# A ranked start, one pause in the state-space queue, and work moved between engines in a two-layer encoder kernel

## The chip, the cores and the metric

The kernel runs on 1 core of one Trainium2 chip. The time is the device time of one execution, in microseconds (us); a number of a kernel is the median over its runs. All data enter and leave in float32. The engines are called TensorE (PE in the rows), VectorE (DVE), ScalarE (ACT), GpSimd (POOL) and SyncE (SP); SyncE starts most DMA transfers, GpSimd starts some.

## The reference

Two sequences, 512 and 256 tokens of width 2048, pass through two layers. The even layer runs a state-space mixer (two directions, 64 groups of 16 channels, 64 states) with a gated linear unit, beside an attention of 8 heads over 2 key/value heads; the odd layer runs 16 heads of attention in which three windows are mixed. Each ends with an out-projection, a residual and a layer norm.

```python
def trunk(x):
    ...
    for layer in range(DEPTH):
        i = layer // 2
        if layer % 2 == 0:
            h = x @ even_w_in[i]
            a_u, a_g, q, k, v, b_g = jnp.split(h, EVEN_SPLITS, axis=-1)
            ya = _s5_mixer(a_u, ...)
            yb = _axial_gqa(q, k, v, attn_q_norm[i], attn_k_norm[i], row, col)
            y = jnp.concatenate([ya * jax.nn.silu(a_g), yb * jax.nn.silu(b_g)], axis=-1) @ even_w_out[i]
        else:
            h = x @ odd_w_in[i]
            q, k, v, g = jnp.split(h, 4, axis=-1)
            y = (_dilated_mixture(q, k, v, pos) * jax.nn.silu(g)) @ odd_w_out[i]
        x = _layernorm(DN_ALPHA * x + y, ln_g[layer], ln_b[layer])
    return x
y_prompt = trunk(x_prompt)
y_sample = trunk(x_sample)
```

In the mixer, `y = gelu(state-space output)`, then `y * sigmoid(y @ glu_w + glu_b)`. The attention normalises q and k per head, rotates them (rope), takes a softmax over all keys and sums the values.

## The kernel before

All 768 tokens are kept on chip with features on the 128 partitions, so a projection runs over weight blocks of 128 x 512 and streams 384 (or 256, 512) columns per matmul. Float32 operands are split into a rounded high part (a cast on ScalarE, L441 or L447) and a low part (the difference, on VectorE or GpSimd, L442 or L448); each product is three matmuls, high by high, high by low and low by high.

The order of the work is written by hand. Projections (`proj_f`, L536; `proj_t`, L580) call `fill` after every block of matmuls: 24 of 384 columns in `proj_f` (6 with `fine`), 36 of 256 columns in `proj_t`. A fill takes the next entry of a queue `c.q` (or a `nop`, which is a pause of one fill) and everything that `later` has set down for that count. What is in the queue runs between the matmuls: TensorE's part of it stands in TensorE's program at that place, and VectorE, ScalarE and GpSimd get theirs through their own in-order programs. `flush` empties the queue at once. A scheduler puts each engine's instructions in order by a modelled time and a rank; `high_priority(n)` raises the rank of what is created in it, `issue_after(i)` holds an instruction behind another.

The stages that the change touches, in order of time:

- **Start** (`load_x`, `before`): x is transposed on TensorE (`ps_x`), cast on ScalarE (`xh`) and its low parts are taken on VectorE (`xl`), while both engines also work out the state-space tables (`pi`, `ui`, `tt`, L137 to L160).
- **State space** (`Ssm`, eight batches b): `inward` makes `swb`, `bb`, `swbb` and `win`, `outward` makes `swc` and `ca`; `ends` turns them on TensorE (`ps_w`, `ps_s`), `cmat` gives `cst` (through `ps_c`), `lags` gives `ps_k`, `scan` is a long chain on VectorE that ends with the two copies to `xb` (L394), and `outs` (`ps_y`, L409 to L412) uses the scan one batch later. `gate` multiplies a projection's two banks into `gt` on VectorE (L682).
- **k and q blocks** (`qk_block`): norm on VectorE, rope as sine products (L669, VectorE), cosine products (L672, GpSimd) and their sum (L673, VectorE), then transposes on TensorE (`ps_q`, L648). Key, value and query of a head are then loaded and split (`load_kv`, `Head0.load`).
- **First attention** beside the glu products: a `step` of the attention (scores `ps_sc`, softmax on VectorE and ScalarE, transposes `ps_pt`, values `ps_o`) is one queue entry.
- **Start of the second layer**: the layer-normed rows z are turned (`four`), sums and differences of quarters are formed (`sums`, L1208), and the first products of a seven-product scheme run alone (`sv.alone`).
- **Last out-projection**: the last heads of the second attention run between its matmuls; each k block of the mixed heads is loaded (`md`) and split (`mix_in`, L1447), the gates (`g`, Tanh, L1439) are loaded through `pd`, and the first 256 columns of the residual (`res0`) are loaded from `nd` and get the layer norm's gain and offset (`residual1`, L1350).

## Time and profile before

| | |
|---|---|
| median of 3 runs | 2634.8 us (2634.49 to 2635.05) |
| profiled execution | 2632.97 us |
| its span in the trace | 2631.2 us |
| TensorE busy | 2541.3 us, 97% |
| VectorE busy | 1787.2 us, 68% |
| ScalarE busy | 1050.0 us, 40% |
| GpSimd busy | 772.5 us, 29% |
[...]

Busy time is summed per engine over the span. [...] The trace has about 90 us in which TensorE does nothing, most of it in a few waits.

### The profile page before, as it was taken

How to read it: one execution, taken by the hardware profiler on the slowest of the kernel's cores; microseconds unless marked ns; L12 is line 12 of the kernel's file. 1: busy time of each engine (PE TensorE's matmuls, PEld its weight loads, DVE VectorE, ACT ScalarE, POOL GpSimd, SP SyncE). 2: the span in 40 equal slices, each digit the busy share in tenths (PEclk: the TensorE clock that was granted, in tenths of full speed). 3: DMA queues.
4: the chain of work that ended last, by engine and by line, in shares of the span. 5: the costliest groups of instructions: out<-in, count | busy, mean ns of one | idle time of the engine just before them, and what ended most of it. 6: DMA issues, size and time to landing. Idle time of an engine off the chain costs nothing.

```text
span 2631.2 us, 41939 instructions
## 1 busy us (share of the span) xinstructions
PE 2541.3 (97%) x15632; PEld 2432.2 (92%) x15632; DVE 1787.2 (68%) x3516; ACT 1050.0 (40%) x2102; POOL 772.5 (29%) x641
## 2 busy tenths in 40 slices
PE   7999999999999999998999999999999999989996
PEld 7999999999988998888999999999999999988886
DVE  6488998878445542238866666778788878763437
ACT  4322233222237731117433333456555656651111
POOL 2555666645564420004000000012212212244404
PEclk9999999999999999999999999999999999989998
DMA  5433333332354462125443444454544454456222
GB/s 154 124 88 99 96 98 97 102 88 71 110 150 141 142 207 64 64 89 165 138 131 124 129 126 127 137 117 111 119 115 109 112 117 113 101 163 196 77 74 106
DMA packets 353451, 308.59 MB, mean 117 GB/s; under 512 B 60384, under 2 KB 305120, under 8 KB 352352
## 3 DMA queue, kind: packets, MB, share of 16 engines
q1 hardware_dynamic: 333200, 265.83, 33.3%
q0 software_dynamic: 10688, 36.71, 6.9%
q10 hardware_dynamic: 9360, 3.38, 0.7%
q8 instruction: 123, 2.02, 0.3%
q14 instruction: 80, 0.66, 0.1%
HBM read 232.10 MB, written 67.44 MB: 114 GB/s over the span
## 4 chain that ended last, share of the span: by engine, by line
PE 70%; DVE 16%; DMA 4%; issue 3%; POOL 2%; ACT 1%; SPq 0%; DVEq 0%; POOLq 0%; ACTq 0%
PE pt L580 23%; PE ps_y L753 12%; PE ps_z L753 8%; PE ps_x L753 8%; PE pa L536 4%; PE pb L536 4%; PE ps_o L885 3%; PE ps_sc L843 2%; DMA res<-pd 2%; PE ps_pt L872 2%; DVE wl L442 1%; DVE tmpv L227 1%; DVE xs L370 1%; PE ps_y L410 1%; DVE sc_sw L369 1%
## 5 line engine op out<-in xcount | busy, mean ns | idle before, releaser
L441 ACT CAST wh<-wr 128x512 fp32r<-128x512 f32 x348 | 216.3, 622 | 715.3 <-PE pt L580 391.5
L580 PE MATMUL pt<-wh,xh 128*128 128x256 f32 (+1 forms) x1392 | 458.8, 330 | 0.9 <-DVE z L898 0.8
L580 PE MATMUL pt<-wl,xh 128*128 128x256 f32 (+1 forms) x1392 | 456.1, 328 | 0.0
L580 PE MATMUL pt<-wh,xl 128*128 128x256 f32 (+1 forms) x1392 | 455.9, 327 | 0.0
L442 POOL TENSOR_TENSOR wl<-wr,wh 128x512 fp32r<-128x512 f32 x176 | 245.1, 1398 | 532.7 <-ACT wh L441 470.0
L442 DVE TENSOR_TENSOR wl<-wr,wh 128x512 fp32r<-128x512 f32 x172 | 145.8, 849 | 257.0 <-ACT wh L441 256.4
L580 PEld LDWEIGHTS pt<-wh,xh 128*128 128x128 f32 x1392 | 265.8, 191 | 25.0 <-issue 2.5
L580 PEld LDWEIGHTS pt<-wl,xh 128*128 128x128 f32 x1392 | 265.8, 191 | 22.3
L580 PEld LDWEIGHTS pt<-wh,xl 128*128 128x128 f32 x1392 | 265.5, 191 | 22.3
L753 PE MATMUL ps_y<-xh,wh 128*128 128x384 f32 x768 | 260.0, 339 | 0.0
L753 PE MATMUL ps_y<-xl,wh 128*128 128x384 f32 x768 | 257.1, 335 | 0.9 <-DVE xl L1208 0.9
L753 PE MATMUL ps_y<-xh,wl 128*128 128x384 f32 x768 | 257.0, 335 | 0.0
L441 ACT CAST wh<-b 128x512 fp32r<-128x512 f32 x248 | 151.6, 619 | 184.4 <-PE ps_z L753 91.5
L442 DVE TENSOR_TENSOR wl<-b,wh 128x512 fp32r<-128x512 f32 x248 | 170.2, 688 | 38.4 <-ACT wh L441 38.2
L753 PE MATMUL ps_x<-xh,wh 128*128 128x384 f32 x512 | 176.1, 344 | 7.5 <-ACT early L761 6.1
L753 PE MATMUL ps_z<-xh,wh 128*128 128x384 f32 x512 | 174.1, 340 | 0.0
L753 PE MATMUL ps_x<-xh,wl 128*128 128x384 f32 x512 | 172.0, 336 | 0.0
L753 PE MATMUL ps_x<-xl,wh 128*128 128x384 f32 x512 | 171.9, 336 | 0.0
L753 PE MATMUL ps_z<-xh,wl 128*128 128x384 f32 x512 | 171.4, 335 | 0.0
L753 PE MATMUL ps_z<-xl,wh 128*128 128x384 f32 x512 | 171.1, 334 | 0.0
L536 PE MATMUL pa<-xh,wh 128*128 128x384 f32 x448 | 158.3, 354 | 4.4 <-ACT xh L447 3.3
L536 PE MATMUL pa<-xh,wl 128*128 128x384 f32 x448 | 151.5, 338 | 0.6 <-POOL wl L442 0.4
(355 smaller groups left out, 6374.7 us busy)
## 6 DMA issues: line engine op xcount, KB each, us to landing
b<-in_odd_w_in_dram SPq DMA_DIRECT2D x256, 256.0 KB, 3.0
wr<-in_even_w_in_dram SPq DMA_DIRECT2D x144, 256.0 KB, 3.3
pd<-z SPq DMA_DIRECT2D x56, 384.0 KB, 2.5
wr<-in_even_w_out_dram SPq DMA_DIRECT2D x64, 256.0 KB, 2.6
wr<-in_odd_w_out_dram SPq DMA_DIRECT2D x64, 256.0 KB, 3.0
res<-pd POOLq DMA_DIRECT2D x16, 768.0 KB, 6.9
res<-pd POOLq DMA_DIRECT2D x16, 576.0 KB, 6.4
nd<-z POOLq DMA_DIRECT2D x12, 512.0 KB, 4.2
```

Source lines behind the costliest of these rows:

```text
L227: e.tensor_tensor(out=tmp, in0=pt(9 + j), in1=xt(sx), op=ALU.mult)
L369: v.tensor_tensor(out=sw, in0=sw, in1=bc(ai), op=ALU.mult)
L370: v.tensor_tensor(out=x1, in0=x1, in1=sw, op=ALU.add)
L410: nc.tensor.matmul(o, s.ca[:, 0, g, 1:9].rearrange("p j c -> p (j c)"), s.xs[:, 0:8, :, g].rearrange("p j r -> p r j"), start=False, stop= ...
L441: cast = nc.scalar.copy(hi, src)
L442: (eng or nc.gpsimd).tensor_tensor(out=lo, in0=src, in1=hi.bitcast(F32), op=ALU.subtract)
L536: nc.tensor.matmul(out[n][s][:, 0:HALF], wt[:, j], xt[k][:, HALF * s:HALF * s + HALF], start=k == k0 and i == 0, stop=k == nk - 1 and i == 2)
L580: nc.tensor.matmul(view[t], xt[k][:, tok], wt[:, j], start=first and i == 0 and ti % per == 0, stop=last and i == 2 and ends)
L753: nc.tensor.matmul(ps, w[:, k], x(k), start=i < 3 and k == j == 0, stop=k == 3 and j == 2, skip_group_check=i >= 3)
L843: nc.tensor.matmul(s, a[:, qs], b[:, ks], start=j == 0, stop=j == 2)
L872: nc.tensor.transpose(ps[:, 128 * j:128 * j + 128], seq.ps[i][:, 128 * j:128 * j + 128], c.ident)
L885: nc.tensor.matmul(o, a, b[:, j], start=j == 0 and x == 0, stop=j == nt - 1 and x == 2)
```

## The change

In the order of the program:

1. Start: the cast and the low part of x in `load_x` are ranked 400 higher.
2. State space: in batch 1 a `nop` is put into the queue behind `ends[1]`, so that all later entries of the state space run one fill later than before against the projections.
3. Before the k and q blocks the `nop` ahead of `tables_in` goes; the cosine products move from GpSimd to VectorE (two of 128 x 256 in each of 15 blocks); the last q block is transposed at fills 2, 3, 4 instead of 1, 2, 3; the low parts of the first key, value and query go from GpSimd to VectorE.
4. First attention: the two fills ahead of the glu loop go.
5. Second layer's start: the products with index 0 run for all four n first, then those with index 3; the last token tile's `four` and `sums` are ranked 400 higher, and the second half of the sums is issued after the first half's last low part.
6. Last out-projection: the gates of the last pair come at fills 5 and 8 instead of 4 and 5, and their Tanh is issued after the attention's cast; the mixed heads are loaded into five buffers of their own four blocks ahead, apart from their splits; the residual's two operations go to VectorE and to block k = 4, its load to k = 9; the extra fills stand at k = 1, 3, 9, 11, 13 and the flush at k = 4.

```diff
 def split_ps(nc, src, hi, lo):
-    nc.scalar.copy(hi, src)
+    cast = nc.scalar.copy(hi, src)
...
+                with c.tc.high_priority(400):
+                    split_ps(nc, ps[:, 0:HALF], c.xh[k][:, tok], c.xl[k][:, tok])
...
-            nc.gpsimd.tensor_tensor(out=o, in0=u, in1=cg[:, 2 * i + tt].unsqueeze(1).to_broadcast([128, 2, 128]), op=ALU.mult)
+            nc.vector.tensor_tensor(out=o, in0=u, in1=cg[:, 2 * i + tt].unsqueeze(1).to_broadcast([128, 2, 128]), op=ALU.mult)
...
-                        ends[1],
+                        ends[1]]
+                    if b == 1:
+                        c.q.append(nop)
+                    c.q += [
...
-            c.q += [nop] + [tables_in, k_part, nop, nop, o[0], o[1], o[2], o[3]]
+            c.q += [tables_in, k_part, nop, nop, o[0], o[1], o[2], o[3]]
...
-                load_split(pk, kd[kv], *k, 3)
-                load_split(pk, vd[kv].rearrange("p t f -> p (t f)"), *v, 3)
+                eng = None if kv else nc.vector
+                load_split(pk, kd[kv], *k, 3, eng)
+                load_split(pk, vd[kv].rearrange("p t f -> p (t f)"), *v, 3, eng)
...
-            q_block(3, at=(1, 2, 3))
+            q_block(3, at=(2, 3, 4))
...
-            fill(c, 2)
             for f in range(8):
                 ps = proj_f(c, [(glu_w[0], 128 * f)], 8, fine=True)[0]
...
                     def more():
-                        tt(a12, a12, a11, ALU.subtract)
+                        with tc.issue_after(last[-1].ins):
+                            tt(a12, a12, a11, ALU.subtract)
                         split(parts[2:])
...
+                else:
+                    c.q += [lambda f=f: ranked(f) for f in ks((4, 0)) + [sums]]
+                    late.extend(ks((8, 12)))
...
-                for n in range(n_first):
-                    for i in (0, 3):
+                for i in (0, 3):
+                    for n in range(n_first):
                         sv.alone(n, i, lambda: fill(c, 2))
...
-                        later(c, 4 + i, lambda i=i: gate_sb(blocks[i], two[i], i))
+                        later(c, 4 + i if n < 31 else 5 + 3 * i, lambda i=i: gate_sb(blocks[i], two[i], i))
...
-                nc.scalar.activation(out=g, in_=t, func=AF.Tanh, scale=0.5)
+                with tc.issue_after(att.cast):
+                    nc.scalar.activation(out=g, in_=t, func=AF.Tanh, scale=0.5)
...
+            def mix_load(k, raw=None):
+                if k < 15:
+                    mixed[k] = pm.tile([128, TOK], F32, tag="mi", name="mi", bufs=5) if raw is None else raw
+                    nc.sync.dma_start(mixed[k], md[k])
...
             def mix_in(k):
                 if k < 15:
-                    raw = pc.tile([128, 4, HALF], F32, tag="res", name="res", bufs=3).rearrange("p a n -> p (a n)")[:, 0:TOK]
-                    nc.sync.dma_start(raw, md[k])
-                    split_sb(nc, raw, c.xh[k], c.xl[k], nc.vector)
+                    with tc.issue_after(att.cast):
+                        split_sb(nc, mixed[k], c.xh[k], c.xl[k], nc.vector)
...
-            nc.sync.dma_start(res0, nd[:, :, 0:256])
-            residual1(pc, res0, 0)
...
-            for k in order1[:3]:
+            for k in order1[:2]:
+                mix_load(k, first[:, TOK * k:TOK * k + TOK])
                 mix_in(k)
+            for k in order1[2:4]:
+                mix_load(k)
...
-                m = order1.index(k) + 3
-                if k in (1, 3, 9):
+                m = order1.index(k)
+                if k in (1, 3, 9, 11, 13):
                     fill(c)
-                if k == 10:
+                if m < 12:
+                    mix_load(order1[m + 4])
+                if m < 14:
+                    mix_in(order1[m + 2])
+                if k == 9:
+                    nc.sync.dma_start(res0, nd[:, :, 0:256])
+                if k == 4:
                     flush(c)
-                if m < 16:
-                    mix_in(order1[m])
+                    residual1(pm, res0, 0, nc.vector)
```

What this does to the engines' programs is seen at three places. The first is VectorE behind the first scan, whose end is the copy to `xb`; `gt` is the gate, `swc` and `tmpv` belong to the output matrix, `swb`, `bb`, `swbb` and `win` to the input matrix of the next batch. Before:

```order
L394 COPY xb<-xs 128x8x32
L682 SCALAR_TENSOR_TENSOR gt<-gt,pa 128x384
L682 SCALAR_TENSOR_TENSOR gt<-gt,pb 128x384
L258 STREAM_SHUFFLE swc<-cst 128x256
L227 TENSOR_TENSOR tmpv<-st,swc 128x576
L236 STREAM_SHUFFLE swb<-bst 128x128
L243 TENSOR_TENSOR bb<-st,bst 128x256
L242 TENSOR_TENSOR bb_1993<-st,swb 128x256
L244 TENSOR_TENSOR bb<-bb,bb_1993 128x256
L246 STREAM_SHUFFLE swbb<-bb 128x256
L228 TENSOR_TENSOR win<-st,bb 128x512 x2
```

Now:

```order
L394 COPY xb<-xs 128x8x32
L684 SCALAR_TENSOR_TENSOR gt<-gt,pa 128x384
L684 SCALAR_TENSOR_TENSOR gt<-gt,pb 128x384
L236 STREAM_SHUFFLE swb<-bst 128x128
L243 TENSOR_TENSOR bb<-st,bst 128x256
L242 TENSOR_TENSOR bb_2023<-st,swb 128x256
L244 TENSOR_TENSOR bb<-bb,bb_2023 128x256
L246 STREAM_SHUFFLE swbb<-bb 128x256
L258 STREAM_SHUFFLE swc<-cst 128x256
L228 TENSOR_TENSOR win<-st,bb 128x512
L227 TENSOR_TENSOR tmpv<-st,swc 128x576
L228 TENSOR_TENSOR win<-st,bb 128x512
```

The five operations from `swb` to `swbb` stood behind `swc` and `tmpv`; now they stand ahead of both.

The second place is VectorE behind the next scan (L391 is the scan's last sum); the same names, and in the batches after it the rows read the same way. Before:

```order
L391 TENSOR_TENSOR xs<-xs,sc_f_2258 128x7x48
L394 COPY xb<-xs 128x8x32
L682 SCALAR_TENSOR_TENSOR gt<-gt,pa 128x384
L682 SCALAR_TENSOR_TENSOR gt<-gt,pb 128x384
L236 STREAM_SHUFFLE swb<-bst 128x128
L243 TENSOR_TENSOR bb<-st,bst 128x256
L242 TENSOR_TENSOR bb_2707<-st,swb 128x256
L244 TENSOR_TENSOR bb<-bb,bb_2707 128x256
L246 STREAM_SHUFFLE swbb<-bb 128x256
L228 TENSOR_TENSOR win<-st,bb 128x512 x2
L258 STREAM_SHUFFLE swc<-cst 128x256
L227 TENSOR_TENSOR tmpv<-st,swc 128x576
```

Now:

```order
L391 TENSOR_TENSOR xs<-xs,sc_f_2295 128x7x48
L684 SCALAR_TENSOR_TENSOR gt<-gt,pa 128x384
L394 COPY xb<-xs 128x8x32
L684 SCALAR_TENSOR_TENSOR gt<-gt,pb 128x384
L242 TENSOR_TENSOR bb_2737<-st,swb 128x256
L243 TENSOR_TENSOR bb<-st,bst 128x256
L244 TENSOR_TENSOR bb<-bb,bb_2737 128x256
L246 STREAM_SHUFFLE swbb<-bb 128x256
L228 TENSOR_TENSOR win<-st,bb 128x512 x2
L236 STREAM_SHUFFLE swb<-bst 128x128
L258 STREAM_SHUFFLE swc<-cst 128x256
L227 TENSOR_TENSOR tmpv<-st,swc 128x576
```

One product of the gate now stands between the scan's last sum and the second copy to `xb`; the `swb` that stood ahead of `bb` was taken an earlier turn, and the next batch's `swb` stands in front of `swc`.

The third place is ScalarE in the last out-projection: `g` is the Tanh of a gate, `pth` the attention's cast, `pp` its softmax, `xh` the cast of a mixed head's block, `o` the copy of an attention output. Before:

```order
L1466 ACTIVATE o_24528<-ps_o 128x256
L447 CAST pth<-ps_pt 128x2x128
L854 ACTIVATE pp<-pp,sst 128x512
L1439 ACTIVATE g_24808<-res 128x768
L441 CAST xh<-res 128x768
L447 CAST pth<-ps_pt 128x2x128
L1439 ACTIVATE g_24852<-res 128x768
L852 ACTIVATE pp,sst<-pp,sst 128x512
L441 CAST xh<-res 128x768
L854 ACTIVATE pp<-pp,sst 128x512
L441 CAST wh<-wr 128x512
```

Now, at the first of the two gates:

```order
L447 CAST pth<-ps_pt 128x4x128
L856 ACTIVATE pp<-pp,sst 128x512
L441 CAST xh<-mi 128x768
L441 CAST wh<-wr 128x512
L447 CAST pth<-ps_pt 128x4x128
L1454 ACTIVATE g_24842<-res 128x768
L854 ACTIVATE pp,sst<-pp,sst 128x512
L441 CAST xh<-mi 128x768
L856 ACTIVATE pp<-pp,sst 128x512
L854 ACTIVATE pp,sst<-pp,sst 128x256
L1487 ACTIVATE o_24898<-ps_o 128x256
```

The gates stood ahead of the next `pth` and, the second, right behind it; now the first of them stands behind two more softmax steps, and the mixed heads' casts read their own buffers `mi`.

## Rows read from the trace of the kernel before

**Rows 1.** which waits TensorE had: us in total, times, the longest
```profile
PE ps_q L648 <- DVE qr L673: 10.9, 4, 5.7
PE ps_y L410 <- DVE xs L391: 8.2, 3, 5.9
PE ps_o L885 <- ACT pth L447: 7.1, 2, 5.3
PE ps_x L753 <- ACT early L761: 6.1, 3, 3.5
...
PE ps_pt L872 <- ACT pp L854: 4.9, 2, 3.7
PE ps_sc L843 <- DVE kl L442: 4.7, 4, 3.3
PE ps_x L603 <- DVE xl L448: 4.4, 2, 2.8
PE pa L536 <- ACT xh L447: 3.3, 1, 3.3
```

**Rows 2.** Stretches: us; busy PE, PEld, DVE, ACT, POOL; granted clock; DMA share; GB/s
```profile
20.00:45.00 25.00, 17.34 (x107) 16.14 (x105) 24.04 (x90) 12.56 (x29) 9.13 (x10) 0.93 0.54 121
160.00:245.00 85.00, 77.00 (x480) 76.16 (x479) 72.66 (x168) 22.73 (x45) 40.53 (x29) 0.92 0.39 102
270.00:290.00 20.00, 20.00 (x118) 20.00 (x117) 19.39 (x64) 4.23 (x9) 8.67 (x7) 1.00 0.48 119
626.00:633.00 7.00, 7.00 (x61) 7.00 (x60) 5.74 (x10) 1.49 (x3) 5.41 (x7) 1.00 0.14 40
640.00:656.00 16.00, 10.35 (x77) 10.14 (x77) 11.81 (x20) 4.67 (x9) 10.76 (x12) 0.89 0.28 73
745.00:802.00 57.00, 46.82 (x253) 44.45 (x253) 29.71 (x48) 27.99 (x53) 32.39 (x24) 0.92 0.51 162
1210.00:1250.00 40.00, 33.00 (x180) 31.24 (x179) 36.18 (x54) 27.14 (x63) 12.51 (x12) 0.91 0.56 168
2312.00:2360.00 48.00, 37.16 (x244) 35.30 (x243) 31.44 (x49) 29.13 (x58) 22.50 (x15) 0.86 0.60 177
```

**Rows 3.** timeline of ScalarE, start of the kernel: start, us, line, out<-in, count, wait
```profile
36.39 2.52 ACT L151 ACTIVATE tt<-pi 64x576 f32<-64x576 f32 x4 [5.12 <-DVE pi L143]
```

**Rows 4.** timeline of VectorE and TensorE around the state-space batches
```profile
176.50 0.01 DVE L258 LOAD_MASK_SELECT swc<-cst  x1 [6.86 <-ACT cst L220]
...
177.70 0.30 DVE L236 STREAM_SHUFFLE swb<-bst 128x128 f32<-128x128 f32 x1
...
179.97 0.44 DVE L246 STREAM_SHUFFLE swbb<-bb 128x256 f32<-128x256 f32 x1
...
365.48 0.58 PE L410 MATMUL ps_y<-xs,ca 128*128 128x96 f32 x2 [0.24 <-DVE xs L391]
365.76 0.55 DVE L682 SCALAR_TENSOR_TENSOR gt<-gt,pa 128x384 f32<-128x384 f32 x1
```

**Rows 5.** k and q blocks: operations by line and shape, 675 to 692 us
```profile
L669 DVE TENSOR_TENSOR qsq<-qn,qks 128x128 f32<-128x128 f32 x12 | 7.4, 674 | 0.0
L672 POOL TENSOR_TENSOR qr<-qn,qkc 128x256 f32<-128x256 f32 x6 | 4.6, 785 | 2.2 <-DVE qn L663 2.2
```

**Rows 6.** timeline around the last scan, and VectorE before the last q block
```profile
609.38 0.39 DVE L394 COPY xb<-xs 128x256 f32<-128x256 f32 x1
...
614.80 0.36 PE L409 MATMUL ps_y<-ug,mtoep 128*128 128x96 f32 x2
...
745.31 0.69 DVE L660 TENSOR_REDUCE qss<-qsq 128x4 f32<-128x512 f32 x1 [17.05 <-ACT qsq L658]
```

**Rows 7.** timeline at the head of the last out-projection
```profile
2314.83 5.48 DVE L442 TENSOR_TENSOR ql<-res,qh 128x768 fp32r<-128x768 f32 x1 [1.17 <-ACT qh L441]
2315.97 3.52 POOL L1350 TENSOR_TENSOR res<-res,lrow 128x1536 f32<-128x1536 f32 x1
...
2334.95 0.84 ACT L1439 ACTIVATE g<-res 128x768 f32<-128x768 f32 x1 [3.33 <-DMA res<-pd]
```

## Prediction of the time after the change

> **What bounds the kernel now.** TensorE works 2541.3 of the span's 2631.2 us (the table), so there is little to be had but its waits and its half clock. I read its waits first [rows 1]. The reader is to see eight groups that make 49.6 us, nearly all of them in stretches that the change touches (of the 4.7 only the longest, 3.3), and that each has one or two long waits. Then the same stretches with the granted clock [rows 2]. One less the clock, times the length, is what a stretch loses to the half level: 0.07 x 25 = 1.8 us at the start, 0.08 x 85 = 6.8 in the state space, 0.11 x 16 = 1.8 and 0.08 x 57 = 4.6 around the q blocks and the first attention, 0.09 x 40 = 3.6 at the second layer's start, 0.14 x 48 = 6.7 in the last out-projection: 25.3 us. Two stretches without waits have the full level, 1.00 [rows 2]. So the clock falls where TensorE has waited, and a wait that goes can give its loss back. At stake are some 73 us, no more. Last I read the timeline at each place, for what ends the wait [rows 3 to 7].
>
> Prices of a fill: 24 matmuls of 384 columns at 20.00 / 118 = 0.17 us make 4.1 us; 36 of 256 columns at 7.00 / 61 = 0.115 also 4.1; six of the glu products 1.0 [rows 2].
>
> **Part 1, start.** Three waits, 4.4 in two and 3.3 [rows 1]. The last four casts of x stood behind four multiplies of 2.52 / 4 = 0.63 us [rows 3] and now stand behind three of them; the low parts move by about as much. But VectorE is busy 24.04 of 25 us here [rows 2]: the rank makes no time, it puts table work behind x. Nothing gained to all 7.7 gained; I take -2.0, three times the 0.63, with the clock unchanged.
>
> **Part 2, state space.** (a) The first `ps_y` waits 5.9 us for the scan [rows 1]. The scan does not move, TensorE has one fill more to do until then: -4.1, and 1.8 stays. (b) Of 8.2 some 2.1 are left for the second `ps_y` (0.24 is a third). VectorE stood idle 6.86 us ahead of `swc`, and did `swb` to `swbb` behind it, 177.70 to 180.41 [rows 4]; now these 2.7 us fall into the idle time: the wait goes, -2.0 (0 if `bst` lands late). (c) Clock: with one wait gone and one cut to 1.8 I count 4.4 of the 6.8. (d) In five later batches a gate product of 0.55 us slips between the scan's last sum and the second copy to `xb`. There is nothing to spare: in one of these batches TensorE already waits 0.24 for the scan [rows 4]. So 5 x 0.5 = +2.5 (0 to 2.8). Together -8.0.
>
> **Part 3, k and q blocks.** By TensorE's program the last batch's `ps_s` now stands behind 2652 projection matmuls (2616 before) and its `ps_y` behind 2877 (2904 before): 63 fewer lie between, 7.2 us. The scan was done at 609.77 and used at 614.80 [rows 6], 5.0 us to spare: a new wait of 2.2 (0 to 3.5). The wait of 5.7 at the first q block's end is that of the same VectorE chain, which starts one fill later. On it go two cosine products a block: not shown on VectorE; between less than nothing (L669, 0.67 us on the mean for 128 columns, is stretched beside GpSimd's products) and GpSimd's 0.785 [rows 5]; I take 0.4, near the copy of 256 columns to `xb`, 0.39 [rows 6], and as much back. So little changes: -1.0 with the clock, between -7.5 (both gone) and +4.
>
> [...]
>
> The last q block has the other 5.2 of the 10.9 [rows 1]. Its three transposes come one fill, 4.1 us, later, while VectorE ends as before: all 5.2 go, and 1.4 of the clock: -6.6. The three low parts cost nothing: even at 5.48 us each, the slowest of their width [rows 7], they would fill 16.4 of the 17.05 us in which VectorE stood idle [rows 6].
>
> **Part 4, first attention.** `ps_pt` waits 4.9 us in two [rows 1] for a softmax without matmuls beside it. Without the two fills, two of the steps get six glu matmuls between them: -2.0, and half of the 3.2 us of clock that the q block leaves: -1.5. The attention ends two fills later, with fewer glu products to cover its last values: +1.4 (0 to 2.0). Together -2.1.
>
> **Part 5, second layer's start.** The 6.1 us in three waits [rows 1] are those of the products with index 3, which now come later. But VectorE is busy 36.18 of 40 us [rows 2] and the next products need its low parts: TensorE waits there in their place. I take -2.0 (0 to -9.7, the waits and the clock).
>
> **Part 6, last out-projection.** (a) `ps_sc` waits 3.3 us: `ql` took 5.48 us on VectorE around the residual's 3.52 on GpSimd [rows 7], and `kl` came behind it. The residual leaves that place. But the first mixed block is now cast behind `kh` and a softmax step, and TensorE needs it for its first matmul: by two casts of the 0.84 of `g`'s width [rows 7] about 1.8 of wait, -1.5. (b) ScalarE stood 3.33 us for a gate's load [rows 7] with `pth` behind it, and TensorE 5.3 [rows 1]. The gates come later, behind `pth`: -5.2. (c) The other wait for `pth`, 1.8, has a whole half block of 18 matmuls in front of it now: -1.8. (d) The residual on VectorE, 1536 columns twice: between 2.2 us (four times the 0.55 of 384 columns [rows 4]) and GpSimd's 3.52; 2.2 taken. Behind it stands the softmax of the next step, and two half blocks of 18 matmuls, 4.1 us, cover most: +1.0. (e) Clock: 4.9 of 6.7. Together -12.4.
>
> [...]
>
> **Sum.** -2.0 - 8.0 - 1.0 - 6.6 - 2.1 - 2.0 - 12.4 = -34.1 us. The profiled execution took 2632.97 us (1.8 around the span) and would take 2598.9. The median lies 1.8 above the profiled execution: 2600.7.
>
> **Rivals.** First, handed back: VectorE's chains set the end in parts 2 to 5, and every half-clock stretch stays. Then -1 at the start, -4.1 - 1.5 + 2.5 in the state space, -5.2 + 2.2 in the q blocks, nothing in parts 4 and 5, -7.5 in the last: -14.6, 2620. For it: VectorE's busy shares [rows 2]; against it: long waits that end on a load or on GpSimd have nothing to do with these chains.
>
> Second, the out-projection keeps its waits: the residual's load now stands behind seven loads on SyncE, and if it lands late VectorE stops ahead of a softmax; the gain of 12.4 is lost: -21.7, 2613. For it: one load held ScalarE 3.33 us [rows 7]. Against it: the first softmax behind it is due a half block later.
>
> Third, slower: from the third batch on `swb` stands in front of `swc` and waits for `bst`, which SyncE loads only after `bb` has read the buffer; and the chain has nothing to spare [rows 4]. In six batches the loss is six times what VectorE's idle time there does not cover; from 5.7 us a batch on it eats the 34.1. At the 6.86 us that VectorE once waited at this place [rows 4] it is +41.2 - 34.1 = +7.1: 2642. Against it: the wait was for `cst`, and `ca` behind it waits for `ps_y` anyway.
>
> **How the numbers follow.** The forecast has 0.58, the first rival 0.20, the second 0.12, the third 0.07, and 0.03 that parts cancel to no change. About 0.2%, 5.3 us, is what a measurement of this kernel can tell from no change. A quarter of the first rival falls within it: faster 0.58 + 0.15 + 0.12 = 0.85, same 0.08, slower 0.07. The range goes up to 2622, just past the first rival, and down to 2584: with the unknown bounds at parts 1, 3 and 5 in the kernel's favour by half (2.9 + 3.2 + 3.9) and the rest of the clock in parts 2 and 6 (4.2) and in part 4 another 1.5.
>
> **What would show it.** In the trace after: the first `ps_y` waits under 2 us and the second not at all, `swbb` ends ahead of `swc`; `ps_y` of the last batch waits about 2; the last q block's transposes and the `pth` behind the gates wait for nothing; the first matmul of the last out-projection waits for `xh`; the clock at 1.00 around the second `ps_y` and the last q block. I am wrong if the waits of rows 1 come back under other names with the same sum, or if `ps_y` waits for the scan in each batch.

## The result and the profile after

The changed kernel took 2607.04 us (median of four runs, 2604.1 to 2610.74), the kernel before 2634.64 beside it (2631.41 to 2635.05). The ratio is 0.9899, with a 95% interval of 0.9881 to 0.9916: 27.6 us less, where 2600.7 us had been forecast, in a range of 2584 to 2622. The profiled execution took 2610.74 us, the slowest of the four, with a span of 2608.7. So the two traces differ by 22.5 us and the medians by 27.6; terms of one or two microseconds can't be read from the medians, and I read them from the traces, stage by stage. Of the 22.5 us, 5.3 are TensorE's busy time (2541.3 before, 2536.0 now, for the same 15632 matmuls; the mean granted clock is 0.986 before and 0.988 now, and one less the clock, times the span, is 36.8 and 31.3 us, so by my estimate this is nearly all clock), and 17.2 its idle time (89.9 before, 72.7 now).

First TensorE's waits, by what ended them (us in total, times, longest), as in [rows 1]:

```profile
PE ps_y L755 <- ACT wh L441: 6.9, 2, 6.6
PE ps_y L410 <- DVE xs L391: 6.4, 3, 2.7
...
PE pt L581 <- ACT xh L441: 4.5, 1, 4.5
PE pa L537 <- ACT xh L447: 3.5, 2, 3.3
PE ps_q L650 <- DVE qr L675: 3.3, 1, 3.3
PE ps_o L887 <- DVE ptl L448: 3.1, 1, 3.1
...
PE ps_x L604 <- DVE xl L448: 2.9, 2, 2.5
PE ps_y L412 <- DVE xb L394: 2.9, 4, 1.2
...
PE ps_pt L874 <- ACT pp L856: 1.7, 1, 1.7
```

The reader is to see what is gone and what is new. Gone are the wait for `pth` (7.1), that for the copies into `early` (6.1), two thirds of that for `qr` (10.9 to 3.3) and of that for `pp` (4.9 to 1.7). New are 6.6 us for a weight cast at the second layer's start, 4.5 for a cast of `xh` and one wait of 3.1 for `ptl` in the last out-projection. The kernel before had waits for `ptl` too, but six short ones:

```profile
PE ps_o L885 <- DVE ptl L448: 5.4, 6, 1.3
```

The waits for the scan are not less, they sit elsewhere: 8.2 before, now 6.4 for `xs` and 2.9 for `xb`, the copies at the scan's end.

Then the stretches, with the columns of [rows 2]; the last one is the out-projection, which lies some 15 us earlier now:

```profile
160.00:245.00 85.00, 82.15 (x533) 81.03 (x532) 72.91 (x168) 24.52 (x48) 43.85 (x30) 0.98 0.42 106
290.00:320.00 30.00, 27.32 (x174) 26.81 (x173) 21.47 (x49) 10.28 (x19) 14.53 (x11) 0.94 0.44 113
640.00:656.00 16.00, 16.00 (x137) 16.00 (x136) 12.42 (x23) 4.43 (x8) 9.54 (x9) 1.00 0.47 116
...
2295.00:2345.00 50.00, 42.11 (x310) 40.50 (x310) 33.77 (x53) 32.20 (x63) 15.74 (x15) 0.97 0.66 191
```

TensorE is busier where the change meant it to be (82.15 of 85 us against 77.00, and 16.00 of 16 against 10.35, at a clock of 0.98 and 1.00). But 290 to 320 us now has a hole of 2.7 us and a clock of 0.94, where the kernel before had neither:

```profile
290.00:320.00 30.00, 29.94 (x200) 29.58 (x199) 24.22 (x58) 10.57 (x20) 15.63 (x12) 1.00 0.46 124
```

In both traces the granted clock stands at 1.00 or at 0.50 (0.50 in each microsecond from 174 to 177 of the changed kernel's); a value between is a mean over the stretch, and half clock here means the 0.50.

Last, the stages. TensorE does the same matmuls in both kernels, so I take the moment at which it starts the same one (the 606th projection matmul, the last matmul of a stage, and so on) and see how much earlier it comes than before. The difference from one such moment to the next is what the stage gained. "Again" is a second profiled execution of the changed kernel, from the first experiment:

| stage (us in the kernel before) | forecast | after | again |
|---|---|---|---|
| start, to 154 | -2.0 | +2.6 | +0.8 |
| state space, k and first q block, to 659 | -9.0 | -4.2 | -3.3 |
| last q block, first attention, to 946 | -8.7 | -9.5 | -11.8 |
| second layer's start, to 1267 | -2.0 | +1.1 | +0.8 |
| second layer, to 2316 | 0 | -4.1 | -3.8 |
| last out-projection, to 2368 | -12.4 | -6.7 | -4.4 |
| rest | 0 | -1.7 | -1.7 |
| sum | -34.1 | -22.5 | -23.4 |

The direction was right, four terms were too good by 3 to 8 us each, and 5.8 us came from the two stages for which nothing had been forecast; the experiments ask why.

### The profile page after: what moved, and what is told of

Read it like the earlier page. It is cut to its first block, busy times and chain, and to the rows that moved or that the text cites. A ratio compares the mean times of both kernels' runs of the same rounds, so it can differ in the third digit from the quotient of the medians.

```text
span 2608.7 us, 41911 instructions
## 1 busy us (share of the span) xinstructions
PE 2536.0 (97%) x15632; PEld 2430.6 (93%) x15632; DVE 1782.9 (68%) x3551; ACT 1048.8 (40%) x2102; POOL 735.7 (28%) x606
## 4 chain that ended last, share of the span: by engine, by line
PE 76%; DVE 17%; issue 2%; DMA 2%; POOL 2%; ACT 1%; SPq 0%; DVEq 0%; ACTq 0%; POOLq 0%
PE pt L581 25%; PE ps_y L755 14%; PE ps_z L755 9%; PE ps_x L755 9%; PE pa L537 3%; PE pb L537 3%; PE ps_o L887 3%; PE ps_sc L845 3%; PE ps_pt L874 2%; DVE tmpv L227 1%; DVE xs L370 1%; DVE sc_p L367 1%; DVE sc_sw L369 1%; DVE sc_sw L366 1%; PE ps_y L410 1%
## 5 line engine op out<-in xcount | busy, mean ns | idle before, releaser
L442 DVE TENSOR_TENSOR wl<-wr,wh 128x512 fp32r<-128x512 f32 x172 | 137.9, 803 | 260.2 <-ACT wh L441 259.8
L1421 POOL DMA_DIRECT2D rt<-res x64 | 32.9, 514 | 718.0 <-DMA cos<-in_c_rope_dram 476.7
```

What stands on the lines that cost most here:

```text
L442: (eng or nc.gpsimd).tensor_tensor(out=lo, in0=src, in1=hi.bitcast(F32), op=ALU.subtract)
L1421: nc.gpsimd.dma_start(rt[32 * i:32 * i + 32], t[0:32, i])
```

## The experiments

Each kernel was timed against the kernel before on one chip. Intervals of the ratio are about 0.0035 wide, 9 us, so a single edit of 3 us shows in a trace and seldom in a median.

**The changed kernel again**, unaltered.

> The changed kernel once more, unaltered, as the measure for the others of this chip. Every theory expects 2607 us (2604 to 2611) and in its profile the same waits of TensorE at the same places: 2.7 before the first ps_y at 171 us, none before the second, 2.5 at 302, 6.6 at 1226, 4.5 at 2307 and 3.1 at 2322. A wait that moves by more than 0.5 us from one execution to the next is no evidence in the other runs.

2608.55 us (2600.56 to 2609.76, five runs), ratio 0.9901 [0.9885, 0.9916]. The five waits that I had named came back at their places within about 0.6 us (2.5, 2.5, 6.7, 5.1, 2.7); the 5.1 in place of 4.5 moved by more than the 0.5 set before, so small changes of that wait prove nothing. The wait of 1.2 at 432 us, which the next two expectations name, didn't come back. The stretches of half clock moved more than the waits did: after the first `ps_y` 6.8 us instead of 3.4, and a new one of 3.4 near 2320. Stage by stage the two executions differ by up to 2.3 us, and the later executions of the same code by more: that is the noise of the table above.

**No pause** in the second state-space batch:

```diff
-                    if b == 1:
-                        c.q.append(nop)
```

> The pause in the second state-space batch is taken out, all else stays. Theory A, the pause buys the first two waits and costs the later batches: the first ps_y waits 5 to 6 us again (2.7 with the pause) and the second about 2 (0), while the waits at 302, 432 and 498 us (2.5, 1.2, 1.2) and their half-clock stretches at 303 and 433 go; from 240 to 600 us TensorE gains back about 8.6 us and the whole is the same within 3 us, 2604 to 2610. Rival B, the later batches wait for another reason (the gate product ahead of the second copy of the scan, whatever the phase): the waits at 302 and 432 stay, and the whole is slower by the 4 to 8 us of the first two batches, 2611 to 2615.

2603.77 us (2598.08 to 2605.94), 0.9886 [0.9870, 0.9901], at the lower end of what theory A expects. The first `ps_y` waits 5.70 again and the second 2.41, and from 250 to 600 us the distance to the kernel before stays at 3.0 us; the waits at 302 and 498 us are gone (the one at 432 proves nothing). State space and first q block gain 9.3 us in this trace, against 4.2 and 3.3 with the pause. That gap is too good: the first two combined versions below, which leave the pause out as well, gain 4.9 and 6.1 in this stage. What all traces show is the loss from the second batch's `ps_y` to the seventh's, measured against the kernel before: 6.6 to 12.5 us in the seven executions that carry the pause along with GpSimd's low parts, and 0.0, 4.2 and 1.1 in the three without the pause. By the median the pause costs 3 to 5 us, though the intervals still overlap.

**Pause for one batch only**: the next batch's first two pieces share a step, so all later ones have their old place.

```diff
+                    c.q += [lambda r=rows: (r[0](), r[1]())] if b == 2 else rows[:2]
```

> The pause stays, but the first two pieces of the third batch are issued in one step instead of two, so that only the second batch runs one fill later and from the third on each piece stands beside the same fill as before the change. Theory A: the first ps_y still waits 2 to 3 us and the second not at all, the waits at 302, 432 and 498 us go with their two half-clock stretches (1.7 us each), from 240 to 600 us some 6 to 8 us less than with the pause carried along, 2599 to 2602. Rival B (two pieces in one step): the transposes of both halves fall together, TensorE waits there for copies of the first, 2 to 4 us, and half or more of the gain is lost, 2603 to 2607. Rival C (the waits come from the gate product, not the phase): they stay, 2607.

2601.1 us (2598.85 to 2606.89), 0.9882 [0.9866, 0.9899]. Of the three later waits the one of 2.5 at 302 us is down to 1.2, another of 1.2 stands a batch later, and the rest is gone: most of them comes with the phase of the batches, as A says. From the second batch to the seventh 2.4 us are lost. But the second `ps_y` waits 3.17 again, so the stage gains 7.9, no more than without a pause.

What the phase changes can be read from VectorE's chain, from its first `ca` product to the second copy into `xb`. In the kernel before and in the run without the pause it takes 51.1 to 51.9 us in the third to sixth batch, with ten or eleven low parts of the weights on GpSimd that reach into it. In the changed kernel it takes 54.5, 51.2, 53.0 and 53.0, with twelve, ten, eleven and eleven; in its second execution two of the four have 53.0 or more. A gate product slips into all four, also into the one of 51.2: it alone doesn't make a chain late. Nor is it the pause alone, since without it the first combined version has 53.0 in three of the four. Here is the end of the chain of 54.5, the timeline of the changed kernel (start, us, instruction, idle time before it):

```profile
299.98 1.35 POOL L442 TENSOR_TENSOR wl<-wr,wh 128x512 fp32r<-128x512 f32 x1 [2.90 <-ACT wh L441]
300.12 1.67 DVE L394 COPY xb<-xs 128x512 f32<-128x512 f32 x1
301.70 0.50 DVE L391 TENSOR_TENSOR xs<-xs,sc_f 128x336 f32<-128x336 f32 x1
302.12 0.54 DVE L684 SCALAR_TENSOR_TENSOR gt<-gt,pa 128x384 f32<-128x384 f32 x1
302.25 0.58 PE L410 MATMUL ps_y<-xs,ca 128*128 128x96 f32 x2 [2.50 <-DVE xs L391]
302.59 0.37 DVE L394 COPY xb<-xs 128x256 f32<-128x256 f32 x1
```

The gate product that I had counted at 0.5 is there, ahead of the second copy. But the larger piece is the first copy: it begins 0.14 us after a low part on GpSimd and takes 1.67 us, ending 0.46 after the low part does; in the chain of 51.2 it takes 0.61. In the two chains of 53.0 it is the second copy that meets a low part, 1.34 and 1.37 us in place of 0.37. One such meeting is 1 us, twice the gate product.

**Low parts on VectorE** in the state space, pause kept:

```diff
+                c.weng = nc.vector
                 ssm.load(0)
...
+            c.weng = nc.gpsimd
             o = ssm.outs(7, store_y)
```

> One edit on the changed kernel, with the pause kept: in the eight state-space batches the low parts of the weights (wl, 128x512) are made by VectorE, not by GpSimd; the k and q blocks keep GpSimd. In the traces VectorE's chain from ca to the second copy into xb takes 51.1 to 51.9 us with ten low parts of GpSimd beside it, 53.0 with eleven, 57.0 with twelve in the first batch: each one beside it costs 1.1 to 1.9 us, while on VectorE it takes 0.68. Theory A (the low parts stretch the chain by more than their own work): the chain falls to 44 to 48 us, the waits for ps_y at 171, 302, 432, 498 and 615 us (2.7, 2.5, 1.2, 1.2, 1.2) go with their half clock (1.7 each), 2594 to 2600. Rival B: a low part now stands behind VectorE's chain and TensorE waits for wl in each batch, 0.5 to 1 us a fill in some fills: 2605 to 2625. Rival C: the chain's length has other reasons (the count of low parts goes along with its length only): it grows by ten times 0.68, 58 us, and ps_y waits 6 us more in each batch, 2650.

2601.7 us (2599.0 to 2606.67), 0.9886 [0.9869, 0.9902]. Theory A by its mechanism, with a total 1.7 us above its range: the chain takes 45.5 to 47.1 us in the second to seventh batch although nine low parts are on VectorE itself (and, with a chain so short, the gate product no longer slips in). Two groups (busy, mean ns | idle) in the fifth batch's chain, first without the pause and with GpSimd's low parts, then with VectorE's:

```profile
L442 POOL TENSOR_TENSOR wl<-wr,wh 128x512 fp32r<-128x512 f32 x10 | 15.5, 1558 | 16.5 <-ACT wh L441 16.5
L367 DVE TENSOR_TENSOR sc_p<-xs,st 128x192 f32<-128x192 f32 x7 | 4.1, 588 | 0.0
```

```profile
L442 DVE TENSOR_TENSOR wl<-wr,wh 128x512 fp32r<-128x512 f32 x9 | 8.1, 900 | 0.0
...
L367 DVE TENSOR_TENSOR sc_p<-xs,st 128x192 f32<-128x192 f32 x7 | 2.4, 347 | 0.0
```

A scan product takes 347 ns instead of 588 on the mean, and the whole chain is 4 us shorter with more work in it. All waits for the scan go but the last batch's, 1.2 and 0.4, whose chain still has six low parts of GpSimd beside it and takes 42.13 us in both traces (not because of them: in the third combined version it has none and takes 42.2). The stage gains 13.2 us instead of 4.2 and 3.3, and from the second batch to the seventh 2.1 us are lost. What is late next is a transfer:

```profile
232.01 0.43 PE L409 MATMUL ps_y<-ug,mtoep 128*128 128x96 f32 x2 [2.10 <-DMA mtoep<-kd]
```

**Cosine products back on GpSimd**, as before the change:

```diff
-            nc.vector.tensor_tensor(out=o, in0=u, in1=cg[...], op=ALU.mult)
+            nc.gpsimd.tensor_tensor(out=o, in0=u, in1=cg[...], op=ALU.mult)
```

> Only the two cosine products of each block go back to GpSimd. Theory A (they were what stretched VectorE's swapped products and held qr): TensorE waits again 5 to 6 us at the end of the first q block, around 650 us, and again about 5 us in two or three waits around the last q block in place of its one of 3.3: 5 to 9 us slower in all, 2612 to 2616. Rival B (the order of the k part and the later transposes of the last block did it, not the engine): the wait at the first q block stays away and the last block keeps its one wait of 3.3: within 2 us of the changed kernel, 2606 to 2610. Forecast of the prediction: 0.4 us for a product on VectorE and as much back, so no difference by itself.

2610.15 us (2603.94 to 2617.72), 0.9915 [0.9896, 0.9934]. Neither, but a bit of both. At the first q block a wait of 2.06 comes back, not 5 to 6, with 3.4 us of half clock: the stage from 618 to 659 us gains 6.4 instead of 10.2. So the products' engine is worth 3.7 us there, and the order of the k part, by what is left, the rest. At the last q block the one wait is 1.46 here and 3.32 with the products on VectorE, so half of that is lost again. The total shows no difference outside the interval. The first wait and what VectorE and GpSimd did ahead of it:

```profile
648.93 1.98 DVE L671 TENSOR_TENSOR qsq<-qn,qks 128x128 f32<-128x128 f32 x4
649.07 1.50 POOL L674 TENSOR_TENSOR qr<-qn,qkc 128x256 f32<-128x256 f32 x2 [0.90 <-DVE qss L663]
...
652.22 0.69 DVE L675 TENSOR_TENSOR qr<-qr,qsq 128x512 f32<-128x512 f32 x1
...
653.05 1.09 PE L650 MATMUL ps_q<-ident,qr 128*128 128x128 f32 x4 [2.06 <-DVE qr L675]
```

Four small sine products take 1.98 us beside GpSimd's; four of them alone take 0.90 in the changed kernel (at 642.99).

**Start and second layer's start as before** (the casts of x without `high_priority(400)`; the early products by column pair; the last tile's sums without rank):

```diff
-                for i in (0, 3):
-                    for n in range(n_first):
+                for n in range(n_first):
+                    for i in (0, 3):
```

> Two places are put back as before the change, which the trace keeps apart by 1100 us: the casts of x without rank, and the second layer's start (products 0 and 3 of each column pair by turns, the last token tile's sums without rank). Theory A: neither was worth anything. At 150 us the kernel stands within 2 us of the changed one, which in five executions of the same code stood there between 1.4 us earlier and 2.6 later than before; at the second layer's start the one wait of 6.7 us at 1223 to 1226 turns back into the three waits of 1.4, 1.2 and 3.5 with their sum of 6.1, and the half clock there is 6.8 us long either way: the whole 2607 plus or minus 2. Rival B, as forecast: each is worth 2 us, so 2611. Rival C: the rank at the start puts the tables' work behind x and costs, so without it TensorE is 1 to 2 us earlier at 150 us, 2606.

2607.53 us (2604.26 to 2612.44), 0.9904 [0.9888, 0.9920]. Theory A for both. At 154 us this kernel is 0.5 us ahead of the kernel before; twelve executions that have the rank lie between 1.4 ahead and 2.6 behind, 0.2 behind on the mean. At the second layer's start the new wait turns back into the old ones, and the stage gains 1.1 where the change lost 1.1 and 0.8 (in its other executions between 0.5 lost and 0.3 gained):

```profile
PE ps_x L754 <- ACT early L762: 6.1, 3, 3.5
```

**Two rows for the residual** in the last out-projection, so that the row of its sum is loaded before the product runs:

```diff
+            if eng is nc.vector:
+                row_in(ln_g)
+                row_in(ln_b)
...
+                rows[src.name] = pool.tile([128, 256], F32, tag="lrow", name="lrow", bufs=2 if eng is nc.vector else 1)
+                nc.gpsimd.dma_start(rows[src.name], src[0:1, cols].to_broadcast([128, 256]))
```

> The residual of the last out-projection gets two row buffers, so that the row of its sum is loaded before its product runs and not behind it. In the changed kernel VectorE stands 3.2 us for that load at 2316 to 2320 us, with ptl queued behind the sum, and TensorE waits 3.1 (2.7 in the second execution) for ptl at 2322. Theory A: with the row there, the sum follows its product at once, ptl comes 3 us earlier and this wait goes: 2.7 to 3.1 us less at this place, 2604 to 2606. Rival B: the product itself or the softmax step ahead of it is what is late, TensorE waits for pth or the product's chain in its place: 0 to 1 us less, 2607 to 2608.

2606.28 us (2605.36 to 2607.92), 0.9899 [0.9882, 0.9916]. Theory A at its place: the sum follows its product, VectorE doesn't stop, and TensorE's wait for `ptl` is gone. The stage gains 7.7, although the wait at its head was 6.2 in this execution. That is at the upper end of the 4.4 to 7.6 of the seven executions without the edit, so it is the wait that shows the effect, not the sum.

**First mixed blocks cast at once**, not behind the last softmax step's cast:

```diff
-                mix_in(k)
+                mix_in(k, True)
...
+                if k < 15 and free:
+                    split_sb(nc, mixed[k], c.xh[k], c.xl[k], nc.vector)
```

> The first two mixed blocks are cast as soon as they are loaded, not behind the cast of the last softmax step issued before them. Theory A: the first matmul of the last out-projection waits 4.5 us only because the cast of its block is queued behind kh and a softmax step on ScalarE, which stood 5.3 us for a load ahead of the qh cast; cast ahead of these, the wait goes with its half-clock stretch (1.7), 2601 to 2603. Rival B: the load that ScalarE waits for is late all the same, the next softmax step comes as late as before and the wait only moves from the first product to the next transposes or to the second block's low part: 2606 to 2608.

2607.96 us (2606.14 to 2612.05), 0.9908 [0.9893, 0.9922]. Rival B by the total. The wait of 4.5 at the first matmul is gone, and 2.0 for `kh` comes in its place. The stage gained 9.3, more than without the edit, but the median doesn't show it. What stands behind the late load stays late; so the load was next.

**Few loads under way**: two `mi` buffers, not five, each block's cast ahead of the next load, and the residual asked for by ScalarE behind `kh`.

```diff
-                    mixed[k] = pm.tile([128, TOK], F32, tag="mi", name="mi", bufs=5) if raw is None else raw
+                    mixed[k] = pm.tile([128, TOK], F32, tag="mi", name="mi", bufs=2) if raw is None else raw
...
-                if k == 9:
-                    nc.sync.dma_start(res0, nd[:, :, 0:256])
+                if k == 0:
+                    with tc.issue_after(att.cast):
+                        nc.scalar.dma_start(res0, nd[:, :, 0:256])
```

> One edit on the changed kernel: of the mixed blocks only four are on their way at a time (two of the mi buffers, not five), and the 768 KB of the residual are asked for by ScalarE behind the kh cast, not by SyncE right behind the mi loads. The small res<-rt transfers (48 KB) took 1.8 us to land before the change and 8.0 in the changed kernel, where five mi loads of 384 KB (7.1 us each, 3.8 before) and the residual's (10.4, 4.9 before) are under way; qh's cast stood 5.3 us for them and TensorE 4.5 to 6.2 at the first matmul of the out-projection. Theory A, the loads ahead hold the small ones: res<-rt lands in 2 to 3 us, qh's cast waits under 1, the wait at the first matmul is at most 1.8 as forecast: 3 to 5 us less at that place and up to 3.4 more of half clock, 2599 to 2604. Rival B, res<-rt is slow for another reason (the 576 KB that GpSimd's own queue adds to res, or the weights): it stays at 7 to 8 us and so does the wait, 2606 to 2608. Rival C: with fewer buffers a later mixed block comes late and TensorE waits for it in the middle of the half blocks, 2605 to 2610.

2602.47 us (2599.27 to 2604.38), 0.9890 [0.9871, 0.9909]. Theory A. The DMA issues at the out-projection's head (queue, count, KB each, median us from issue to landing), first of the kernel before, then of the changed kernel, then of this one:

```profile
res<-nd SPq DMA_DIRECT2D x1, 768.0 KB, 4.9
...
res<-rt POOLq DMA_DIRECT2D x4, 48.0 KB, 1.8
```

```profile
mi<-md SPq DMA_DIRECT2D x5, 384.0 KB, 7.1
...
res<-nd SPq DMA_DIRECT2D x1, 768.0 KB, 10.4
...
res<-rt POOLq DMA_DIRECT2D x4, 48.0 KB, 8.0
```

```profile
mi<-md SPq DMA_DIRECT2D x3, 384.0 KB, 4.7
...
res<-nd ACTq DMA_DIRECT2D x1, 768.0 KB, 4.9
...
res<-rt POOLq DMA_DIRECT2D x4, 48.0 KB, 4.0
```

The four small transfers that put the rotated rows back for the last head's q and k took 1.8 us, then 8.0 behind six large ones, and 4.0 here. The `qh` cast waits 1.33 for them instead of 5.31, the first matmul 0.56 instead of 4.53, and the wait of 3.1 for `ptl` is down to 0.9 in two (with a new 1.1 for `pth`), and all half clock of the stage is gone. It gains 12.3 us, near the 12.4 of the forecast, but the rest behind it gains nothing where the changed kernel gains 1.7. The edit changes three things at once (the loads under way, the order of cast and load, the residual's queue and moment), and no run takes them apart. The 4.0 is still above 1.8; why was not tried.

**Combined, first**: no pause, two rows, early casts, five column pairs ahead (and, to make room for the fifth, the tile of the layer norm's statistics in another pool), the second head's q low part on VectorE.

```diff
-            n_first = 4
+            n_first = 5
...
-                    load_split(pk, qd[self.h], *self.qq, 3, None if self.h else nc.vector)
+                    load_split(pk, qd[self.h], *self.qq, 3, None if self.h > 1 else nc.vector)
```

> Five edits on the changed kernel: no pause in the second state-space batch; two row buffers for the last residual; the first two mixed blocks cast as soon as they are loaded; the second head's q low part on VectorE and not on GpSimd, where it took 2.29 us and stretched VectorE's products of the last q block from 0.28 to 1.82 and 0.41 to 1.48; and five column pairs instead of four whose products 0 and 3 are made ahead in the second layer, which puts 24 matmuls, 4.6 us, in front of the wait of 6.7 us. Expected of each by the traces so far: the pause 5 us, the rows 2.9, the casts 2 (4.5 less the 2.0 that came in its place), the low part 2.5 (3.3 less the 0.7 that it takes on VectorE), the fifth pair 4.6 of the wait. If all add up: 2607 - 17 = 2590, with half clock that goes too 2587. Rival: in each of these places VectorE or a load is late next and half comes back: 2598. Rival for the fifth pair: the matmuls move but VectorE's sums move with them, since its own chain starts behind the same loads: 6.7 stays.

2597.41 us (2594.11 to 2599.41), 0.9863 [0.9845, 0.9881], the rival's value of 2598 rather than 2590. The fifth pair works: the wait of 6.6 is 2.78, and the second layer's start gains 2.7. In the last q block 3.32 only became 2.42, because the low part stood ahead of the last `qr` sum, and that sum now met a low part of the weights on GpSimd (1.75 us instead of 0.69).

**Combined, second**: the first, with few loads, and the q low part behind that sum.

```diff
+                with c.tc.issue_after(c.turned.ins):
+                    nc.vector.tensor_tensor(out=lo, in0=raw, in1=hi.bitcast(F32), op=ALU.subtract)
```

Here `c.turned` is the last sum of `qr`.

> The first combined version with two more edits: the few loads of the other run of this call, and the second head's q low part placed behind the last sum of qr on VectorE, not ahead of it (0.94 us, and the sum behind it was stretched from 0.69 to 1.75 by a low part on GpSimd). Expected: the wait of 2.4 us in the last q block falls to 0.5 or less, the wait of 3.3 us for kh ahead of the out-projection to under 1, with half clock of 3.4 us each: 2597 - 2 - 2.5 - 3 = 2590 (2587 to 2594). Rival: the first falls but the second is only moved (the softmax behind kh ends last): 2594 to 2596.

2592.75 us (2586.73 to 2594.46), 0.9846 [0.9827, 0.9866]: the best version, 40 us under the kernel before, with an interval that lies below that of the changed kernel. The last q block's wait is 0.60:

```profile
756.26 0.69 DVE L675 TENSOR_TENSOR qr<-qr,qsq 128x512 f32<-128x512 f32 x1
756.87 0.95 DVE L1071 TENSOR_TENSOR ql<-ld,qh 128x768 fp32r<-128x768 f32 x1
...
757.10 0.63 PE L650 MATMUL ps_q<-ident,qr 128*128 128x128 f32 x4 [0.60 <-DVE qr L675]
```

**Combined, third**: the second, with the low parts on VectorE in the state space, k and q blocks.

```diff
+                c.weng = nc.vector
                 ssm.load(0)
...
             late_gate(15, 3584 + 128 * 7)
             flush(c)
+            c.weng = nc.gpsimd
```

> The second combined version, and with it the low parts of the weights on VectorE in the state space and in the k and q blocks too. Theory A as in the other run of this call: of the second combined version's waits 5.6 and 2.3 us for the first two ps_y go with 6.8 us of their half clock twice (3.4 each in time), and the scan has time to spare in each batch: 2593 - 8 - 5 = 2580 (2578 to 2586); in the q blocks, where VectorE ends last as well, nothing is lost. Rival B: VectorE is now the engine that ends last in the q blocks, since each block has four low parts of 0.68 more on it: 2 to 6 us are lost there, 2584 to 2588. Rival C: TensorE waits for wl throughout: slower than 2593.

2600.14 us (2596.43 to 2604.9), 0.9874 [0.9859, 0.9890]: slower than the second version, as C says, but not by C's mechanism, for TensorE hardly waits for `wl` (0.7 us in the state space). The chain is 46.6 us long, but without the pause `ps_y` now comes before its `mtoep` is loaded and waits for that four times, 1.6 to 3.7 us. Of the 10.8 us between the two traces 6.3 are lost in the second layer, which gave 4.7 back here and gained 1.6 there with the same code, and 2.8 in the last q block and first attention, with a new wait of 2.3 at a score; why is open for both. The pause together with low parts on VectorE, on top of the second version, was not run.

## Why the prediction was right or wrong

**Start, -2.0: nothing came of it, by the prediction's own doubt.** The rank makes no time on a VectorE that is busy 23.71 of the 25 us from 20 to 45 us now. It only changes which transposes wait: 2.5 and 3.3 now, 2.8, 1.6 and 3.3 before. The 2.6 us lost in the first trace are noise: over the twelve executions with the rank it is 0.2.

**State space. The mechanism at the first two `ps_y` was right.** The first waits 2.71 (forecast 1.8, and under 2 as a sign), the second not at all, at a clock of 0.98. **The failed step is (d), the later batches at +2.5.** From the second batch's `ps_y` to the seventh's TensorE lost 8.6 us in the changed kernel's first trace. I had priced the gate product that slips into the chain, 0.5 us, which is there, and had taken the rest of the chain as fixed. It isn't: which of its instructions meet GpSimd's low parts depends on the phase between batch and fill, and one more copy to `xb` that meets one costs 1 us. Two kinds of run show it: without the pause the loss is 0.0 to 4.2 us instead of 6.6 to 12.5, and with the low parts elsewhere it is 2.1, with the pause kept. The phase is not all of it, for without the pause single chains are late too. Half clock came with the new waits (0.94 from 290 to 320 us).

**The third rival's mechanism was there and cost nothing**, for the reason that the prediction gave. VectorE stops ahead of `swb`, 2.2 to 4.2 us in four of the batches, but `ca` waits another 1.6 to 4.8 us for `ps_y` in any case:

```profile
245.33 0.01 DVE L236 LOAD_MASK_SELECT swb<-bst  x1 [4.19 <-DMA bst<-in_ssm_b_im_dram]
...
248.49 3.03 DVE L228 TENSOR_TENSOR ca<-st,cst 128x576 f32<-128x576 f32 x2 [1.60 <-PE ps_y L412]
```

**k and first q block, -1.0: too small.** The wait in the last batch is 1.6 (forecast 2.2), but the 5.7 at the first q block, of which I expected little, is gone altogether; as in the upper bound of -7.5, against which stands 1.7 us lost to half clock behind the new wait (3.41 us of it from 617.36). The product on VectorE costs what I took (0.414 us in the median of the 30, taken 0.4). What I gave back too little for is its neighbours: [rows 5] shows the sine products at 674 ns beside GpSimd, and they take about 0.28 without it (their median in the changed kernel). With the products back on GpSimd 2.1 of the 5.7 returns.

**Last q block, -6.6 with all waits gone: one of 3.3 stayed.** The step said "VectorE ends as before". It ends later, because the second head's q low part is on GpSimd at just this point (in the kernel before it stood a little later, at 762.16, beside the last sum):

```profile
758.13 2.29 POOL L442 TENSOR_TENSOR ql<-ld,qh 128x768 fp32r<-128x768 f32 x1
758.76 3.51 DVE L671 TENSOR_TENSOR qsq<-qn,qks 128x128 f32<-128x128 f32 x4
...
762.19 1.81 DVE L674 TENSOR_TENSOR qr<-qn,qkc 128x256 f32<-128x256 f32 x2
...
764.88 1.08 PE L650 MATMUL ps_q<-ident,qr 128*128 128x128 f32 x4 [3.32 <-DVE qr L675]
```

Put behind the sum on VectorE, it leaves 0.60. **First attention, -2.1**: the wait for `pp` fell from 4.9 to 1.7 with its half clock. That the two parts together gained 9.5 and 11.8 for the 8.7 forecast is luck. Parted at the projection matmul that starts at 775.8 us in the kernel before, the q block gained 1.2 and 2.6 of its 6.6, and the attention 8.3 and 9.2 instead of 2.1. There the waits for `pp` fell by 3.2 and 4.0 (2.0 taken), its 6.8 us of half clock went whole (3.4 us, 1.5 taken), and from 830 us to the end 0.3 us were lost (1.4 taken); the rest stays open, and no run puts the two fills back.

**Second layer's start, -2.0: nothing came of it**, by the argument that the prediction itself gave for doubt. VectorE's sums end last, without a pause from 1213 us on, and one wait of 6.6 stands in place of three with a sum of 6.1:

```profile
1224.07 0.68 DVE L730 TENSOR_TENSOR bt<-b,b 128x512 f32<-128x512 f32 x1
...
1225.08 0.62 ACT L441 CAST wh<-bt 128x512 fp32r<-128x512 f32 x1
...
1225.75 0.69 PE L755 MATMUL ps_y<-xh,wh 128*128 128x384 f32 x1 [6.62 <-ACT wh L441]
```

Undoing the edit is no worse, and five column pairs ahead, which give TensorE other work, take 4 us of it.

**Last out-projection, -12.4: the mechanisms were right, two terms failed.** Terms (b) and (c), the waits for `pth` of 5.3 and 1.8, are gone. Term (a) expected 1.8 us for the first mixed block, from two casts; it was 4.5, for the load ahead of the casts:

```profile
2302.86 0.83 ACT L441 CAST qh<-res 128x768 fp32r<-128x768 f32 x1 [5.31 <-DMA res<-rt]
2304.57 0.83 ACT L441 CAST kh<-res 128x768 fp32r<-128x768 f32 x1
...
2305.71 1.55 ACT L441 CAST xh<-res 128x768 fp32r<-128x768 f32 x2
...
2306.59 0.39 PE L581 MATMUL pt<-wh,xh 128*128 128x256 f32 x1 [4.53 <-ACT xh L441]
```

I had priced the moved loads only where they are waited for, and not what they do to other transfers in flight. Term (d), +1.0 for the residual on VectorE, was 3.1: an operation took 1.75 us, less than the 2.2 taken, but the second one stood 3.19 for its row:

```profile
2312.73 1.75 DVE L1364 TENSOR_TENSOR res<-res,lrow 128x1536 f32<-128x1536 f32 x1
...
2319.55 1.76 DVE L1364 TENSOR_TENSOR res<-res,lrow 128x1536 f32<-128x1536 f32 x1 [3.19 <-DMA lrow<-in_ln_b_dram]
```

That is the second rival's mechanism, with a row of 128 KB in place of the residual. Both terms have their run: with few loads the stage gives 12.3, and with two rows the wait for `ptl` is gone.

**The clock gave back less than the sum took.** The terms that name it, 4.4 + 1.4 + 1.5 + 4.9, make 12.2 us; TensorE's busy time fell by 5.3. A wait that went gave its loss back (at the first two `ps_y` 13.7 us of half clock became 3.4 in the first trace), but the waits that came brought stretches of 3.4 us of their own, at 303, 433 and 617 us.

**Not foreseen** are 4.1 us in the second layer, where code and order of the products are the same, and 1.7 in the rest behind the last out-projection. In the thirteen executions after the kernel before the second layer lies between -6.8 and +4.7; no run isolates it, and one execution of the kernel before is a narrow base. Without these 5.8 us the traces would differ by 16.7, so that the time came out as near to the forecast as it did is in part luck. Between the profiled executions the forecast misses by 11.8 us (2598.9 against 2610.74), between the medians by 6.3; of the 5.5 between, 3.7 are the execution that was profiled, above the median of its four, and 1.8 what the prediction added from the profiled execution to the median.

## What to carry to other kernels

When work is shifted by one step against a periodic loop, the price isn't the one instruction that slips in (0.5 us here, against 1 us for each copy that met a low part): look at which instructions of the critical chain now meet the second engine's, in every later period. Before giving elementwise work to GpSimd, ask whether VectorE is the engine waited for: here a chain with ten low parts on GpSimd beside it took 51.1 us, and 47.1 with nine of them on VectorE itself. Whether the whole gains is another matter, as the third combined version shows. And a load that is asked for earlier is not free while small transfers on a chain are in flight (here 8.0 us instead of 1.8); count the bytes under way at that moment.

## What the runs showed of the hardware

In the trace of the run without the pause a product on VectorE that begins inside a low part on GpSimd ends, at 192 columns, 0.21 to 0.22 us behind it. At 266.79 us GpSimd makes two low parts, and VectorE's scan products of 192 columns, 0.35 us when alone (at 271.09), begin beside them:

```profile
266.79 3.11 POOL L442 TENSOR_TENSOR wl<-wr,wh 128x512 fp32r<-128x512 f32 x2
...
268.68 1.44 DVE L369 TENSOR_TENSOR sc_sw<-sc_sw,st 128x192 f32<-128x192 f32 x1
...
271.09 0.35 DVE L367 TENSOR_TENSOR sc_p<-xs,st 128x192 f32<-128x192 f32 x1
```

The second low part ends at 266.79 + 3.11 = 269.90, the product at 268.68 + 1.44 = 270.12, 0.22 later. From 250 to 520 us of this trace all 25 products of this width that begin inside a low part end 0.21 to 0.22 us behind it, whether they began 0.06 or 0.97 us into it; all 24 of 512 columns that begin inside an operation on GpSimd end 0.55 to 0.56 behind it. All ten shuffles of 192 columns keep their 0.37 us and end inside it. The delay goes the other way too: seven of eleven products of 336 columns keep their 0.50 us, and the low part they began in takes 1.7 to 2.5 us instead of 1.3.

From these numbers an estimate of the price of one more low part in the chain of step (d): a product of 192 columns that begins together with a low part of 1.3 us ends after 1.3 + 0.22 in place of 0.35 us, so up to 1.2 us are lost; the copies that met one lost 1.0.

In the changed kernel's first trace eight of the ten waits above 2 us have a stretch of half clock at them, but not always as long a one: at the first `ps_y` a wait of 2.7 came with 3.4 us of it in one execution, and a wait of 2.5 with 6.8 in the next.
